# Six edits in a decoder step: loads of set-up rows, a root, bias products, attention's projections, the convolution's taps, its state output

## The chip, the cores and the metric

The kernel runs on one core of a Trainium2 chip. The metric is device time in microseconds (us) of one execution; lower is better. The core's engines run side by side, each through its own list of instructions in order: TensorE (PE) multiplies, VectorE (DVE), ScalarE (ACT) and GpSimd (POOL) work on elements, and SyncE (SP) mostly issues transfers (DMA). They wait for each other through semaphores.

## What is computed

One inference step of a trunk of four layers over 512 prompt tokens and 8 sample tokens, 1024 channels, in float32. Layers 0 and 3 mix tokens by causal pooling, layer 1 by dilated window attention in three groups, layer 2 by a convolution module; a SwiGLU feed-forward follows each. Cut to the main lines:

```python
def pool_mixer(h, hist, n_past, w_grp, scale):
    # trailing means over 2, 4, 8, 16 positions minus the token, a linear map per channel group, a scale
    ...
def conv_mixer(h, hist, w_in, b_in, w_dw, b_dw, ln_g, ln_b, w_out, b_out):
    a = h @ w_in + b_in
    u = a[..., :D_MODEL] * jax.nn.sigmoid(a[..., D_MODEL:])
    uh = jnp.concatenate([hist.astype(u.dtype), u], axis=1)
    c = lax.conv_general_dilated(uh, w_dw[:, None, :], (1,), 'VALID', ..., feature_group_count=D_MODEL) + b_dw
    ...
    z = (cf - mu) * lax.rsqrt(var + LN_EPS) * ln_g + ln_b
    y = jax.nn.silu(z).astype(h.dtype) @ w_out + b_out
    return y, uh[:, -CONV_HIST:]
...
for i in range(DEPTH):
    ...
    xp = xp + rmsnorm(mixer(rmsnorm(xp, norm_g[i, 0])), norm_g[i, 1])
    xp = xp + rmsnorm(swiglu(rmsnorm(xp, norm_g[i, 2]), w_ffn_in[i], w_ffn_out[i]), norm_g[i, 3])
```

The sample tokens pass through the same layers. The states (last 15 pooling inputs, window keys and values, last 30 convolution inputs) are outputs too.

## The kernel before

**Tiling.** Channels lie on partitions in eight blocks of 128, tokens along the free dimension: columns CA = 0 to 263 (8 sample tokens, 256 prompt tokens) and CB = 264 to 519. A product in float32 is made from parts: a weight is cast to a short float (`wh`, on ACT, L362) and its rest is `wl` (on DVE, L363), an activation likewise into `mh` and `ml`; three matmuls (L391, L392, L393 in `mm3`) give one term. A weight tile of 128 x 1024 (512 KB) is loaded on SP's queue (L352) into one of three `raw` tiles.

**Norms.** `pre_sums` adds the squares of eight blocks into `acc`; `rstat` turns them into a reciprocal root: L178 sums over partitions on PE, L180 takes the root on ACT (with a table load ahead), L183 the reciprocal on DVE, L185 spreads it on PE; `pre_r` (L338) copies it. Each engine's order is set by a scheduler that issues what its own model holds ready, unless the code names what an instruction must stand behind: `behind` does that, and `ROOT_FIRST` says for a sublayer and a column half how many weight casts after a root must stand behind it. The sublayers are numbered 0 to 7 (`self.at`).

**Start.** `load` issues on SP, in order: two x tiles, the pool's bands, eight groups of set-up rows into one tile (norm gains, biases, the 31 rows of `conv_w_dw`), the sample, the pool's state, x tiles 2 and 3. Then `pool` loads its weights (pool_w). `vectors` turns the rows onto partitions (L136) and the sample (L140), pooling means (L613) follow, then products with pool_w. Semaphores for SP's transfers are taken in turn from a set of eight, so a transfer's issue waits for the one eight before it. L544 sums the squares of the x tiles, L558 and L559 make their reciprocal root, L596 casts the sample's part.

**Attention.** Eight head pairs. `attend` is a generator: at each `yield` a budget of `FILL_STEPS` = 72 pieces of projections for the next head pair is dealt out over `ATT_STEPS` places, so that PE has work while softmax runs elsewhere. The lines between weights and values:

```python
        a = self.attn_weights(own)
        next(smp)
        for _ in range(4):
            yield
```

`attn_weights` merges the three groups (POOL copies L965 and L966, DVE L969 to L980, ACT L1006); `attn_values` begins with transposes of the weighted scores (L1012), later ones wait for `tl` (L1017) at L1033.

**Convolution sublayer.** `depthwise_setup` puts the taps together with 32 copies on POOL (L1215, L1216) into `conv_w` and `conv_b`; `depthwise` multiplies them with an identity of 32 columns into `dg` tiles (DVE, L1233) and runs the taps as matmuls (L1239). `sum_blocks` sums the result over channels (L1274), `conv_out` transposes and stores the state (L1264, L1265, L1266), `layer_norm` centres (L1287), squares (L1289, L1292), adds (L1293), scales (L1302, L1304), takes silu (L1305) and splits into `mh` and `ml` (L1307, L1308), and `linear_out` runs the output product, two weights' terms in turn. Hooks are generators that feed-forward sublayers step through beside their products; `conv_state` is one, in `ffn(1)`, the sublayer ahead.

## Time and profile before

| | us |
|---|---|
| median of 3 runs (2581.84 to 2587.22) | 2582.05 |
| profiled execution | 2584.28 |
| its span | 2582.5 |
| PE busy | 2491.2 (96%) |
| DVE busy | 1614.3 (63%) |
| ACT busy | 1229.2 (48%) |
| POOL busy | 449.5 (17%) |

The mean granted TensorE clock was 0.983 of full. The span begins at 0; times in the rows are from there. A wait is idle time of an engine just before an instruction, put down to what released it last by the trace; where that had long been done, it was another.

### The profile page before, as it was taken

Reading aid. Unit: us, or ns where it says so; the run is one execution under the profiler, and the core shown is the slowest. Engines: PE = TensorE matmul, PEld = TensorE weight load, DVE = VectorE, ACT = ScalarE, POOL = GpSimd, SP = SyncE. Lnnn points to the kernel's source line nnn. Section 1 sums busy time; section 2 is a strip of 40 time slices with the busy share of each in tenths; the row PEclk is TensorE's granted clock in tenths of the full one; section 3 lists DMA queues with packets and bytes.
Section 4 is the critical chain, followed back from the end, with each engine's and each line's share of the span. In section 5 each row is a group of like instructions: output and inputs, shape, how many; then the busy total and the mean of one; then the engine's idle time right before and its main releaser. Section 6 shows DMA issues by size and latency. Waiting matters only on the chain.

```text
span 2582.5 us, 51526 instructions
## 1 busy us (share of the span) xinstructions
PE 2491.2 (96%) x20832; PEld 2457.6 (95%) x20832; DVE 1614.3 (63%) x2906; ACT 1229.2 (48%) x2336; POOL 449.5 (17%) x747
## 2 busy tenths in 40 slices
PE   7999999999999999889999999989999998999998
PEld 7899999999999999889999989979999998999998
DVE  5745655667767777677474576467656557747564
ACT  6644434455544545555342353476444336635342
POOL 3100001222333322320000047322000005100002
PEclk8999999999999999999999999989999999999999
DMA  5585543444444554456464421036655432656451
GB/s 147 151 223 158 165 138 108 142 122 142 142 129 129 144 144 128 131 157 180 140 186 116 139 74 42 2 93 172 183 147 164 140 115 69 170 155 180 131 165 58
DMA packets 653435, 349.83 MB, mean 135 GB/s; under 512 B 14864, under 2 KB 649729, under 8 KB 652909
## 3 DMA queue, kind: packets, MB, share of 16 engines
q1 hardware_dynamic: 648996, 338.10, 45.6%
q0 software_dynamic: 1232, 6.06, 0.8%
q8 instruction: 164, 2.69, 0.5%
q10 hardware_dynamic: 2969, 2.37, 0.4%
q14 instruction: 74, 0.61, 0.1%
HBM read 331.87 MB, written 20.68 MB: 137 GB/s over the span
## 4 chain that ended last, share of the span: by engine, by line
PE 46%; POOL 2%; ACT 1%; DVE 1%; DMA 1%; issue 1%; DVEq 0%; ACTq 0%; POOLq 0%; SPq 0%
PE mm L391 14%; PE mm L392 14%; PE mm L393 14%; PE mm L1239 2%; POOL x L238 1%; DMA raw<-in_w_ffn_in_dram 1%; POOL acc L221 1%; POOL conv_w L1215 0%; PE mm L185 0%; ACT wh L362 0%; DVE wl L363 0%; PE mm L1274 0%; ACT sq L220 0%; PE mm L178 0%; DVE ml L317 0%
## 5 line engine op out<-in xcount | busy, mean ns | idle before, releaser
L391 PE MATMUL mm<-mh,wh 128*128 128x264 f32 (+1 forms) x4544 | 1309.7, 290 | 14.5 <-ACT mh L316 5.1
L392 PE MATMUL mm<-ml,wh 128*128 128x264 f32 (+1 forms) x4544 | 1293.8, 285 | 5.1 <-DVE ml L317 4.7
L393 PE MATMUL mm<-mh,wl 128*128 128x264 f32 (+1 forms) x4544 | 1290.0, 284 | 0.7 <-DVE wl L363 0.7
L362 ACT CAST wh<-raw 128x1024 fp32r<-128x1024 f32 (+1 forms) x557 | 573.9, 1036 | 657.7 <-PE mm L392 408.1
L391 PEld LDWEIGHTS mm<-mh,wh 128*128 128x128 f32 x4544 | 864.4, 191 | 20.5 <-ACT mh L316 6.7
L392 PEld LDWEIGHTS mm<-ml,wh 128*128 128x128 f32 x4544 | 867.1, 191 | 8.8 <-DVE ml L317 8.4
L393 PEld LDWEIGHTS mm<-mh,wl 128*128 128x128 f32 x4544 | 865.5, 191 | 1.0 <-DVE wl L363 1.0
L363 DVE TENSOR_TENSOR wl<-raw,wh 128x1024 fp32r<-128x1024 f32 (+1 forms) x557 | 682.0, 1229 | 282.8 <-ACT wh L362 277.3
L391 PE MATMUL mm<-h,wh 128*128 128x264 f32 (+1 forms) x1408 | 399.1, 283 | 0.9 <-DVE pr L1149 0.9
L392 PE MATMUL mm<-h,wh 128*128 128x264 f32 (+1 forms) x1408 | 398.3, 283 | 0.6 <-DVE h L420 0.6
L393 PE MATMUL mm<-h,wl 128*128 128x264 f32 (+1 forms) x1408 | 398.5, 283 | 0.0
L221 POOL TENSOR_TENSOR acc<-acc,sq 128x264 f32<-128x264 f32 (+1 forms) x90 | 79.3, 881 | 1385.8 <-ACT sq L220 1382.7
L391 PEld LDWEIGHTS mm<-h,wh 128*128 128x128 f32 x1408 | 265.7, 189 | 1.7 <-issue 1.3
L392 PEld LDWEIGHTS mm<-h,wh 128*128 128x128 f32 x1408 | 265.7, 189 | 1.1 <-DVE h L420 0.8
L393 PEld LDWEIGHTS mm<-h,wl 128*128 128x128 f32 x1408 | 265.7, 189 | 0.1
L417 DVE TENSOR_TENSOR u<-mm,r 128x264 f32<-128x264 f32 (+1 forms) x176 | 74.9, 426 | 85.4 <-PE mm L393 85.4
L238 POOL TENSOR_TENSOR x<-x,xt 128x264 f32<-128x264 f32 (+1 forms) x111 | 98.1, 908 | 85.3 <-DVE xt L233 83.5
L415 DVE TENSOR_TENSOR g<-mm,r 128x264 f32<-128x264 f32 (+1 forms) x176 | 74.9, 426 | 43.4 <-PE mm L393 39.7
L454 DVE TENSOR_TENSOR y<-mm,y 128x264 f32<-128x264 f32 x64 | 24.0, 429 | 124.5 <-PE mm L393 124.5
L1106 POOL TENSOR_TENSOR skv<-skv,lg 128x576 f32<-128x576 f32 (+1 forms) x48 | 52.7, 1133 | 218.1 <-ACT lg L1099 218.1
L927 ACT ACTIVATE x<-x,own 128x256 f32<-128x256 f32 (+1 forms) x128 | 61.9, 485 | 60.0 <-DVE own L926 60.0
L418 DVE TENSOR_TENSOR u<-u,g 128x264 f32<-128x264 f32 (+1 forms) x176 | 75.7, 434 | 22.7 <-ACT g L416 9.2
(224 smaller groups left out, 2506.6 us busy)
## 6 DMA issues: line engine op xcount, KB each, us to landing
raw<-in_w_ffn_in_dram SPq DMA_DIRECT2D x352, 512.0 KB
raw<-in_w_qkv_dram SPq DMA_DIRECT2D x72, 512.0 KB
raw<-in_w_ffn_out_dram SPq DMA_DIRECT2D x64, 512.0 KB
skv<-in_cache_swa_g_dram SPq DMA_DIRECT2D x32, 512.0 KB
raw<-in_w_ffn_out_dram SPq DMA_DIRECT2D x32, 384.0 KB
out_dram<-tm SPq DMA_DIRECT2D x32, 256.0 KB
raw<-in_conv_w_in_dram SPq DMA_DIRECT2D x16, 512.0 KB
skv<-in_cache_swa_g_dram SPq DMA_DIRECT2D x16, 256.0 KB
```

The lines of the kernel that those rows point to most:

```text
L221: (eng or nc.vector).tensor_add(post[c], post[c], sq)
L238: self.added = nc.gpsimd.tensor_add(xb, xb, t)
L362: whi = nc.scalar.copy(wh, raw)
L363: self.parted = whi, nc.vector.tensor_sub(wl, raw, wh.bitcast(F32))
L391: nc.tensor.matmul(ps, wh[:, k, :], mh, start=first, stop=False)
L392: nc.tensor.matmul(ps, wh[:, k, :], ml, start=False, stop=False)
L393: nc.tensor.matmul(ps, wl[:, k, :], mh, start=False, stop=last)
L415: nc.vector.tensor_mul(g, pg[2 * i], rr[c])
L417: nc.vector.tensor_mul(u, pg[2 * i + 1], rr[c])
L418: nc.vector.tensor_mul(u, u, g)
L927: nc.scalar.activation(pc, pc, AF.Exp, scale=-1.0, bias=stat[:, lay, 0, c:c + 1], accum_out=stat[:, lay, 1, c:c + 1])
L1106: nc.gpsimd.tensor_mul(v4[:, :, h, :], v4[:, :, h, :], lg[:, h, o:o + n, None].to_broadcast([128, n, 64]))
```

## The change

1. **Set-up rows.** The 31 rows of `conv_w_dw` are loaded as 16 and 15. The pool's state and pool_w are issued ahead of x tiles 2 and 3.
2. **Root.** `ROOT_FIRST` gets (1, CB): 4, the second half of the first feed-forward sublayer.
3. **Bias products.** In `bias_setup` the three matmuls are written ahead of the three copies.
4. **Attention.** Five places instead of four between weights and values, `ATT_STEPS` 28 instead of 27. From a head pair's last scores to its first transposes PE now has 108 projection matmuls, before 96; from its beginning 180, before 174. For the last head pair it is 96, before 84.
5. **Taps.** They are put together in `ffn(1)` by a hook behind `conv_state`: two halves, each a memset and 32 smaller copies on POOL into a side tile, then stored by POOL's queue in a DRAM tile `taps`. The convolution loads that with one transfer (128 x 1184, 592 KB) on SP. The bias is column 36 of the same tile. On SP that load stands behind the sixth weight of the sublayer.
6. **State output.** `conv_out` stands behind the last sum of CA, and the layer norm's first part is written ahead of it.

```diff
--- before.py
+++ after.py
@@ -39,8 +39,8 @@
 SQUARES_ON_POOL = {(1, CA): (2, 4, 6), (6, CA): (1, 3, 5, 7)}
 NEAR_END = {1: (), 4: (3,), 5: (2, 3, 6, 7)}
 STEPS = {4: (8, 0, 0, 0)}
-ROOT_FIRST = {(2, CB): 2, (7, CB): 4}
-ATT_STEPS, FILL_STEPS = 27, 72
+ROOT_FIRST = {(1, CB): 4, (2, CB): 2, (7, CB): 4}
+ATT_STEPS, FILL_STEPS = 28, 72
 LAST_STEPS = (1, 3, 5, 11)
 CONV_FILL = {(1, CB): 3, (2, CA): 3, (2, CB): 3, (3, CA): 3, (3, CB): 2}
 SLOTS = ((0, 0, 9), (1, 9, 9), (2, 18, 5))
@@ -120,14 +120,11 @@
             (R_G, I["norm_g"].rearrange("l f d -> (l f) d")), (R_PS, I["pool_scale"]),
             (R_BIN, I["conv_b_in"].rearrange("o (t d) -> (o t) d", t=2)), (R_BDW, I["conv_b_dw"]),
             (R_LNG, I["conv_ln_g"]), (R_LNB, I["conv_ln_b"]), (R_BOUT, I["conv_b_out"]),
-            (R_DW, I["conv_w_dw"].rearrange("o t d -> (o t) d")),
+            (R_DW, I["conv_w_dw"][0, 0:16, :]), (R_DW + 16, I["conv_w_dw"][0, 16:31, :]),
         ):
             nc.sync.dma_start(rows[r0:r0 + ap.shape[0], :], ap)
         nc.sync.dma_start(xs, I["x_sample"].rearrange("b o d -> (b o) d"))
         history = self.pool_history(0)
-        next(history)
-        for t in range(2, 4):
-            nc.sync.dma_start(self.xin[t], I["x_prompt"][0, t * 128:(t + 1) * 128, :])
         self.vec = c.tile([128, NB, NR], F32, name="vec")
 
         def vectors():
@@ -482,7 +479,10 @@
             for t in range(2):
                 self.load_tokens(t)
             begin[0]()
+            next(begin[1])
             st["w"] = weights()
+            for t in range(2, 4):
+                nc.sync.dma_start(self.xin[t], I["x_prompt"][0, t * 128:(t + 1) * 128, :])
         nc.vector.tensor_mul(sg, self.vec[:, :, R_PS + j], self.vec[:, :, post_row])
         self.flush()
         norm_after = 3 if begin else 1
@@ -757,6 +757,7 @@
         ps = self.psum(16, 368)
         for g, o, n in SLOTS:
             nc.tensor.matmul(ps[:, 16 * o:16 * (o + n)], rb[:, 16 * g:16 * g + 16], e2[:33, 16 * o:16 * (o + n)], start=True, stop=True)
+        for g, o, n in SLOTS:
             nc.scalar.copy(so.rearrange("h (k s) -> h k s", k=16)[:, :, o:o + n],
                            ps[:, 16 * o:16 * (o + n)].rearrange("h (k s) -> h k s", k=16))
         nc.scalar.dma_start(self.strip[:, 896:1264], so)
@@ -901,7 +902,7 @@
         yield from self.scores_g12(hp, kv, own, pr[1])
         a = self.attn_weights(own)
         next(smp)
-        for _ in range(4):
+        for _ in range(5):
             yield
         for i, _ in enumerate(self.attn_values(hp, kv, pr, a)):
             if i in (LAST_STEPS if last else (4, 7, 10, 13)):
@@ -1157,7 +1158,10 @@
         self.ul = lp.tile([128, NB, 32], F32, name="conv_ul")
 
         self.u2 = [lp.tile([128, 4, 8 + 128], F32, name=f"conv_u2{i}") for i in range(4)]
-        self.depthwise_setup(lp)
+        self.w2 = lp.tile([128, NB, 4, 37], F32, name="conv_w2")
+        nc.sync.dma_start(self.w2, self.taps)
+        for u2 in self.u2:
+            nc.gpsimd.memset(u2[:, :, 0:8], 0.0)
         rr, ub = {}, {}
         sums = [self.sum_blocks(c) for c in (CA, CB)]
         fill = chain(*(self.depthwise(lp, b) for b in range(NB)))
@@ -1192,28 +1196,34 @@
         for s in sums:
             for _ in range(7):
                 next(s)
-        self.conv_out(j)
         norm = [self.layer_norm(c, s) for c, s in zip((CA, CB), sums)]
+        next(norm[0])
+        with self.behind((self.summed,)):
+            self.conv_out(j)
         for _ in norm[0]:
             pass
         post = self.post(lambda b: self.v(post_row, b))
         self.linear_out(I["conv_w_out"][j], post, next_row, bias_row=R_BOUT, between=norm[1])
 
-    def depthwise_setup(self, lp):
+    def depthwise_setup(self):
+
 
         nc = self.nc
-        self.w2 = lp.tile([128, NB, 4, 36], F32, name="conv_w2")
-        self.b2 = lp.tile([128, NB, 4], F32, name="conv_b2")
-        self.id32 = lp.tile([128, 32], F32, name="conv_id")
+        self.id32 = self.const.tile([128, 32], F32, name="conv_id")
         nc.vector.tensor_reduce(self.id32, self.ident.rearrange("p (b k) -> p k b", b=4), axis=AX.X, op=ALU.add)
-        nc.gpsimd.memset(self.w2, 0.0)
-        for u2 in self.u2:
-            nc.gpsimd.memset(u2[:, :, 0:8], 0.0)
-        for p in range(4):
-            for q in range(4):
-                pp, pq = slice(32 * p, 32 * p + 32), slice(32 * q, 32 * q + 32)
-                nc.gpsimd.tensor_copy(self.w2[pp, :, q, 5 - p:36 - p], self.vec[pq, :, R_DW:R_DW + 31])
-                nc.gpsimd.tensor_copy(self.b2[pp, :, q], self.vec[pq, :, R_BDW])
+        self.taps = self.dram.tile([128, NB, 4, 37], F32, name="taps")
+        for hb in (slice(0, 4), slice(4, 8)):
+            w2 = self.side_tile()[:, :592].rearrange("p (b q k) -> p b q k", b=4, q=4)
+            nc.gpsimd.memset(w2, 0.0)
+            yield
+            for p in range(4):
+                for q in range(4):
+                    pp, pq = slice(32 * p, 32 * p + 32), slice(32 * q, 32 * q + 32)
+                    nc.gpsimd.tensor_copy(w2[pp, :, q, 5 - p:36 - p], self.vec[pq, hb, R_DW:R_DW + 31])
+                    nc.gpsimd.tensor_copy(w2[pp, :, q, 36], self.vec[pq, hb, R_BDW])
+                yield
+            nc.gpsimd.dma_start(self.taps[:, hb], w2)
+            yield
 
     def to_phases(self, b, ub):
 
@@ -1231,7 +1241,7 @@
         for q in range(4):
             d = lp.tile([128, 36, 32], F32, tag="dg", name=self.n("dg"), bufs=6)
             nc.vector.tensor_mul(d, self.id32[:, None, :].to_broadcast([128, 36, 32]),
-                                 self.w2[:, b, q, :, None].to_broadcast([128, 36, 32]))
+                                 self.w2[:, b, q, 0:36, None].to_broadcast([128, 36, 32]))
             dg.append(d)
         ps = self.psum()
         for q in range(4):
@@ -1244,7 +1254,7 @@
         for q in range(4):
             for s in range(4):
                 src = ps[32 * s:32 * s + 32, q * 128:q * 128 + 128].rearrange("c (h n) -> c h n", h=2)
-                dst, bias = yb[32 * q:32 * q + 32, :, 3 - s, :], self.b2[32 * s:32 * s + 32, b, q:q + 1]
+                dst, bias = yb[32 * q:32 * q + 32, :, 3 - s, :], self.w2[32 * s:32 * s + 32, b, q, 36:37]
                 if b >= 6 and s % 2:
                     nc.vector.tensor_scalar(dst, src, bias, None, op0=ALU.add)
                 else:
@@ -1271,7 +1281,7 @@
         for b in range(NB):
             if b == 0:
                 ps = self.total[c] = self.psum(128, hi - lo)
-            self.nc.tensor.matmul(ps, self.ones, self.y[:, b, lo:hi], start=b == 0, stop=b == 7)
+            self.summed = self.nc.tensor.matmul(ps, self.ones, self.y[:, b, lo:hi], start=b == 0, stop=b == 7)
             yield
 
     def layer_norm(self, c, sums):
@@ -1412,7 +1422,7 @@
         net.ffn(0, 3, 4)
     net.attn(5, 6)
     with net.phase(4, 4):
-        net.hooks.append(net.conv_state(0))
+        net.hooks.append(chain(net.conv_state(0), net.depthwise_setup()))
         net.ffn(1, 7, 8)
     net.conv(2, 0, 9, 10)
     with net.phase(4):
```

Three places in the engines' orders. SP at the start, behind the other rows (side_111 is the rows' tile, side_112 the sample, h_110 the x tiles). Before:

```order
L125 DMA side_111<-in_conv_w_dw_dram 31x1024
L126 DMA side_112<-in_x_sample_dram 8x1024
L522 DMA side_126<-in_state_pool_dram 120x1024
L130 DMA h_110<-in_x_prompt_dram 128x1024 x2
L352 DMA raw_188<-in_pool_w_dram 128x8x128
L352 DMA raw_194<-in_pool_w_dram 128x8x128
```

Now:

```order
L125 DMA side_111<-in_conv_w_dw_dram 16x1024
L125 DMA side_111<-in_conv_w_dw_dram 15x1024
L126 DMA side_112<-in_x_sample_dram 8x1024
L522 DMA side_185<-in_state_pool_dram 120x1024
L349 DMA raw_187<-in_pool_w_dram 128x8x128
L349 DMA raw_193<-in_pool_w_dram 128x8x128
L485 DMA h_110<-in_x_prompt_dram 128x1024 x2
```

The rows come in two pieces, and x tiles 2 and 3 moved behind pool_w.

ACT around the root of the first feed-forward sublayer's CB (wh are casts of weights, g and h the gate and its product). Before:

```order
L416 ACTIVATE g_965<-g_965 128x264
L362 CAST wh_1282<-raw_1280 128x1024
L419 CAST h_756<-u_966 128x264
L362 CAST wh_1288<-raw_1286 128x1024
L362 CAST wh_1294<-raw_1292 128x1024
L362 CAST wh_1300<-raw_1298 128x1024
L180 ACT_TABLE_LOAD
L180 ACTIVATE sd_1172<-mm_1171,eps_rms 128x2
```

Now:

```order
L413 ACTIVATE g_966<-g_966 128x264
L416 CAST h_757<-u_967 128x264
L177 ACT_TABLE_LOAD
L177 ACTIVATE sd_1173<-mm_1172,eps_rms 128x2
L359 CAST wh_1283<-raw_1281 128x1024
L335 COPY r_1181<-mm_1172 128x256
L359 CAST wh_1289<-raw_1287 128x1024
L359 CAST wh_1295<-raw_1293 128x1024
```

The root's table load and root moved ahead of the four casts; the fourth now stands nine rows further on.

PE at the beginning of the convolution's output product (mm_20842 and mm_20843, now mm_20881 and mm_20882, are the results of two weights). Before:

```order
L185 MATMUL mm_20769<-ident,rd_20777 128x8
L391 MATMUL mm_20842<-mh,wh_20832 128x264
L391 MATMUL mm_20843<-mh,wh_20838 128x264
L392 MATMUL mm_20842<-ml,wh_20832 128x264
L393 MATMUL mm_20842<-mh,wl_20833 128x264
L392 MATMUL mm_20843<-ml,wh_20838 128x264
L393 MATMUL mm_20843<-mh,wl_20839 128x264
```

Now, at the passage from the first weight to the second:

```order
L388 MATMUL mm_20881<-mh,wh_20871 128x264
L389 MATMUL mm_20881<-ml,wh_20871 128x264
L390 MATMUL mm_20881<-mh,wl_20872 128x264
L388 MATMUL mm_20882<-mh,wh_20877 128x264
L389 MATMUL mm_20882<-ml,wh_20877 128x264
L390 MATMUL mm_20882<-mh,wl_20878 128x264
```

The two weights' terms were taken in turn; now 24 of the first come ahead of 24 of the second.

ACT at the same place (20877 is the second weight, xt and mh the last blocks of the norm). Now:

```order
L1315 ACTIVATE xt_20857<-xt_20857,vec 128x264
L1315 ACTIVATE xt_20863<-xt_20863,vec 128x264
L1317 CAST mh<-xt_20857 128x264
L1317 CAST mh<-xt_20863 128x264
L359 CAST wh_20877<-raw_20875 128x1024
```

The second weight's cast stood ahead of the first silu; now it stands behind the last block.

## Rows read from the trace of the kernel before

**Rows 1.** The page, part 1: busy time, share of the span, instructions.

```profile
PE 2491.2 (96%) x20832; PEld 2457.6 (95%) x20832; DVE 1614.3 (63%) x2906; ACT 1229.2 (48%) x2336; POOL 449.5 (17%) x747
```

**Rows 2.** Waits of PE, whole span: line, releaser, total us, times, longest.

```profile
PE mm L185 <- DVE rd L183: 16.6, 9, 6.0
PE mm L136 <- DMA raw<-in_pool_w_dram: 9.3, 1, 9.3
PE mm L1012 <- ACT x L1006: 8.8, 7, 1.6
PE mm L178 <- DVE acc L1293: 7.1, 2, 6.6
...
PE mm L178 <- DVE acc L331: 4.1, 1, 4.1
PE mm L391 <- ACT mh L1307: 3.9, 1, 3.9
...
PE mm L391 <- DVE mh L596: 1.4, 1, 1.4
...
PE mm L1033 <- DVE tl L1017: 1.0, 2, 0.8
```

**Rows 3.** Stretches: length, busy us (instructions) by engine, granted clock, DMA share, GB/s.

```profile
108.50:115.40 6.90, 5.29 (x25) 5.29 (x26) 5.78 (x11) 6.01 (x9) 0.00 (x0) 0.51 0.75 221
115.40:130.00 14.60, 14.60 (x123) 14.42 (x123) 9.60 (x20) 7.78 (x14) 0.00 (x0) 1.00 0.40 114
...
1525.20:1532.00 6.80, 6.76 (x33) 6.75 (x34) 5.80 (x14) 3.46 (x9) 4.50 (x6) 0.51 0.01 2
...
1698.00:1702.60 4.60, 4.19 (x19) 4.19 (x20) 4.51 (x13) 4.60 (x13) 0.00 (x0) 0.50 0.38 114
```

**Rows 4.** Timeline at the start: start us, length us, instruction, idle before.

```profile
4.81 1.06 ACT L544 ACTIVATE h<-h 128x1024 f32<-128x1024 f32 x1 [2.11 <-DMA h<-in_x_prompt_dram]
...
7.67 0.23 SPq L125 DMA_DIRECT2D side<-in_conv_w_dw_dram  x1
...
17.91 1.07 PE L136 MATMUL mm<-ident,side 55*128 55x55 f32 x8 [9.30 <-DMA raw<-in_pool_w_dram]
```

**Rows 5.** Waits of SP's queue from 0 to 32 us.

```profile
SPq L352 <- DMA side<-in_conv_w_dw_dram: 0.2, 1, 0.2
```

**Rows 6.** Timeline, first feed-forward sublayer, root of CB.

```profile
101.20 0.50 PE L178 MATMUL mm<-ones,acc 128*128 128x2 f32 x4
...
107.24 1.04 ACT L362 CAST wh<-raw 128x1024 fp32r<-128x1024 f32 x1 [1.21 <-DMA raw<-in_w_ffn_in_dram]
108.30 1.28 ACT L180 ACT_TABLE_LOAD   x1
...
110.11 1.22 PE L185 MATMUL mm<-ident,rd 128*128 128x128 f32 x4 [5.96 <-DVE rd L183]
```

**Rows 7.** Timeline, attention, one head pair.

```profile
687.77 3.56 POOL L966 COPY oth<-own 32x4 f32<-32x4 f32 x16
...
695.28 0.84 PE L1012 MATMUL mm<-ident,x 128*128 128x128 f32 x4 [1.53 <-ACT x L1006]
```

**Rows 8.** Timeline, end of the feed-forward sublayer, start of the convolution.

```profile
1504.41 0.28 PE L393 MATMUL mm<-h,wl 128*128 128x256 f32 x1
...
1510.11 1.21 DVE L363 TENSOR_TENSOR wl<-raw,wh 128x1024 fp32r<-128x1024 f32 x1
...
1510.28 1.29 POOL L1215 COPY conv_w<-vec 32x248 f32<-32x248 f32 x1
...
1515.38 0.38 POOL L1215 COPY conv_w<-vec 32x248 f32<-32x248 f32 x1
...
1519.22 1.36 DVE L1233 TENSOR_TENSOR dg<-conv_id,conv_w 128x1152 f32<-128x1152 f32 x1 [3.94 <-POOL conv_w L1215]
```

**Rows 9.** Timeline, layer norm ahead of the convolution's output product.

```profile
1683.81 1.45 DVE L1287 SCALAR_TENSOR_TENSOR y<-mm,y 128x264 f32<-128x264 f32 x4 [2.15 <-PE mm L1274]
...
1694.59 1.04 ACT L362 CAST wh<-raw 128x1024 fp32r<-128x1024 f32 x1 [0.38 <-DMA raw<-in_conv_w_out_dram]
```

## The prediction

> **What bounds the kernel now.** I read the page's busy shares first: TensorE (PE) is busy for 96% of the span [rows 1], so time can only be won where PE stands still or runs at the lower clock, and work on another engine costs something only if PE waits for it. The second view is the list of PE's waits over the whole span [rows 2]. Six of its rows answer to places that the diff edits: the 9.3 us at L136 (set-up rows), the longest 6.0 us of L185 (a root in the first feed-forward sublayer), the 8.8 us at L1012 (seven of attention's eight head pairs), the 4.1 us at L178 for L331 (start of the convolution sublayer), and the 7.1 (longest 6.6) and 3.9 us at L178 and L391 for L1293 and L1307 (the layer norm ahead of the convolution's output product). The third is the table by stretches, with the granted clock [rows 3]. There a wait shows its second price. Right after the 6.0 us wait PE runs at a clock of 0.51 of full, the 1.2 GHz level: 25 matmuls take 5.29 us of work, where the next stretch, at 2.4 GHz, does 123 in 14.60 us, 0.119 us each. Those 25 would have taken 3.0 us, so 2.3 us went to the clock. After the 4.1 us wait it is 33 in 6.76 us, 2.8 us over 33 x 0.119. A wait removed there may give the clock's part back too.
>
> **The change part by part.**
>
> *A, set-up rows.* PE starts L136 at 17.91 us after a wait of 9.30 [rows 4]. The page names a pool_w load, but what it needs is the rows' tile: its last piece, the 31 rows of conv_w_dw (124 KB), was issued at 7.67 [rows 4], and SyncE's queue was still waiting for exactly that transfer just ahead of its issue at 17.6 [rows 5]. So 124 KB took about 9.9 us, while an x tile of 512 KB, issued at 0.75 as the queue's first, is there at 4.81 [rows 4]. In 16 and 15 rows the two pieces are issued by about 8.2. Bounds: if a piece's time goes by its rows, each takes 5 us and the rows are there at 13.2, a gain of 4.7; if they land like other transfers, in 2 to 4 us, they are there at 10.2 to 12.2, a gain of 5.7 to 7.7. I take 10.5, that is 7, since the x tile is eight times the size of a piece and takes 4.
> The Trainium skill ("DMA: Bandwidth & Descriptors", section "Why a DMA increments its semaphore by 16 and not by 1") has a rule for the number of DMA engines: the largest number up to 16 that divides the slowest dimension of both sides, so 31 rows go to one engine and 16 and 15 rows to 16 and 15. By that rule the faster bound holds; the 9.9 us of the trace agree with one engine, and no row here shows a transfer of 15.
> What hides less afterwards: state_pool and the pool weights now go ahead of x tiles 2 and 3. The product behind the pooling, which before waited 1.4 us for L596 [rows 2], now has its reciprocal for those tiles (L559) ahead of L596 on VectorE, so it can start only when the tiles are in. No wait before names them; now 2 MB, four transfers of 512 KB, must be in by the time that the means are done. A = 7, bounds 4 to 8.
>
> *B, the root ahead of the weight casts.* The sums of L178 run at 101.20 for 0.50 us; ScalarE (ACT) does the square root's table load only at 108.30, for 1.28 us, because four casts stand ahead of it in its order and those wait for their loads (the last 1.21 us, at 107.24); PE goes on at 110.11 after 5.96 us [rows 6]. Now the root stands ahead of the four casts. At the latest its table load begins when the sums end, at 101.7: 1.28 for the load, 0.3 for the root, some 0.3 for VectorE's reciprocal give 103.6. PE stopped at 110.11 - 5.96 = 104.15, and its L182 stands four matmuls earlier now, 103.7. So the wait goes, 5.96, and the clock's 2.3 with it. The casts come behind the root; two were waiting for loads anyway, and PE has the products of weights cast before. If two casts are late by a cast each, 2 x 1.04 us come back. B = 8, bounds 5 to 8.3.
>
> *C, bias products.* Three matmuls no longer wait behind a copy of the one ahead. No row of [rows 2] names that line. Up to one copy each might have held PE: 0.3, bounds 0 to 1.
>
> *D, one more place for projections.* In each of eight head pairs the wait is at the first transposes, L1012. It ends with a chain on GpSimd: 16 copies of L966 from 687.77 for 3.56 us, then VectorE and ACT, then PE at 695.28 [rows 7]. That chain hangs on scores far back. Between the last scores and these transposes 96 projection matmuls stood, now 108; counted from the beginning of a head pair it is only 6 more, since the budget went from 27 to 28. If the chain is fixed to the head pair's beginning, each wait shrinks by 6 x 0.119 = 0.71; if to the last scores, by up to 1.43. The last head pair has no later work to draw on, so I count seven: 7 x 0.71 = 5.0. The upper bound is 8.8, all that these waits hold. The lower is 3: later places have 6 matmuls fewer to cover L1033, which waits 1.0 us now [rows 2].
>
> *E, taps put together earlier.* GpSimd's 32 copies at the convolution's start go; the diagonal of L1233 waited 3.94 us for them and started at 1519.22 [rows 8], and behind it the sums that PE awaited for 4.1 [rows 2]. Now one load of 606 KB brings the taps. It stands behind six weights of the sublayer and behind the last h product, which ends near 1504.7 [rows 8]; with the x tile's 4 us for 512 KB [rows 4] and other loads beside it, it lands by 1511, against the 1515.3 at which VectorE was ready (1519.22 less the wait). So the 4.1 goes. Of the 2.8 us of slow clock behind it I count 2, because VectorE is then next: it was busy for 5.80 of 6.80 us in that stretch [rows 3]. E = 6, bounds 3 (the taps or the pushed-back weights late by 3) to 7.
> Where the 32 copies now run, beside the feed-forward sublayer, they meet VectorE's weight work. The trace: a copy of L1215 takes 0.38 us alone and 1.29 when begun just behind a VectorE operation of 1.21, which itself isn't stretched [rows 8]. A copy that comes second waits; the other way round VectorE would lose at most a copy's 0.38.
> The Trainium skill ("SBUF — State Buffer", section "SBUF: two separate sides") has this as a lock: of a GpSimd operation and a VectorE operation with two SBUF inputs, the second to start is blocked for the whole of the first. The trace agrees for the copy; no row shows the reverse. By that rule this part has a price of its own, which is the third rival.
>
> *F, state output behind the sums.* Before, 16 transposes and four copies of the state stood ahead of the last sums; VectorE's first centring began at 1683.81, and a weight's casts (one of 1.04, after a wait for its load, at 1694.59) and splits stood inside the chain to the first product [rows 9]. Now the last sum of CA comes ahead of the transposes, about 1.4 us sooner, and all casts but one stand behind the chain: I put the first product 3.5 us sooner (2 to 4). But the two weights' products are no longer taken in turn. Before, each block of mh and ml fed six matmuls; now 24 of the first weight come, then 24 of the second, whose cast stands behind ACT's last block. ACT does 13 operations in 4.60 us there, fully busy [rows 3]; two are needed per block, so blocks come every 0.7 to 0.8 us, and a block's three matmuls are done in 0.36. The first 24 take some 6.2 us, then the cast, 1.04, and the split, 1.21 like that of [rows 8], lie open, then 22 more matmuls, 2.6: 11.1 us. Before, 19 of the 48 took 4.2 us at the low clock [rows 3] and 29 x 0.119 = 3.5, 7.7. So 3.4 is lost against 3.5 won, and the next pair of weights is loaded later, since the queue now waits for the state's output: about 2 more. F = -2, bounds -5 to +1.5.
>
> **The sum.** 7 + 8 + 0.3 + 5 + 6 - 2 = 24.3 us. The profiled execution took 2584.28 us (span 2582.5 and 1.8 around it); 2560.0 is left. The median of before, 2582.05, lies 2.2 us lower, so I forecast 2582.05 - 24.3 = 2557.8, **2558 us**. With bounds that don't all fall on one side: 2549 to 2567.
>
> **Rivals.**
> 1. *The waits move rather than go*: A's product waits for x tiles behind 2 MB (A = 4), and D's chain shifts with the scores (D = 0). 24.3 - 3 - 5 = 16.3, 2566. For it: everything on GpSimd's chain starts from scores. Against: six matmuls really move ahead. Chance 0.13.
> 2. *More comes back than counted*: D at 8.8, F at +1.5, C at 1: 24.3 + 3.8 + 3.5 + 0.7 = 32.3, 2550, and 2547 with A and B at their upper bounds (1 + 0.3) and 2 more of the clock. For it: slow-clock stretches follow several of these waits. Chance 0.08.
> 3. *The taps' copies hold VectorE*: 32 x 0.38 = 12.2 us if every copy came first and PE felt it. VectorE has spare time in that stretch, and buffers lie between. 2558 + 12 = 2570. Chance 0.04.
> 4. *Slower*: in attention the later places run short. If L1033 waits 1.4 us (the 12 matmuls moved) in each of eight head pairs, and each wait brings a slow stretch like those above, 2.3 us, that is 8 x 3.7 = 30 us, and D's 5 are lost: 2558 + 35 = 2593. It decides when that wait passes the length that brought the low clock elsewhere. Against it: L1033 waits 1.0 us in all, so there is slack. Chance 0.03.
> 5. *The change doesn't do what it says*: 31 rows aren't what L136 waits for and root and taps are still behind a load: 2558 + 7 + 8 + 6 = 2579. Chance 0.02.
>
> **How the numbers follow.** The forecast has 0.70; 2547 to 2569 takes in most of rivals 1 and 2. A measurement of this kernel can tell about 0.2%, 5 us, from no change: faster means below 2576.9. Only rivals 4 and 5 lie outside that: faster 0.94, same 0.03, slower 0.03.
>
> **What would show it.** A: L133 near 10.5, products near 22.5. B: no wait above 1 us at L182 near 104, full clock behind. D: the first L1013 waits 0.7 shorter in each head pair. E: the diagonal not waiting, no 4 us at L175. F: products of the first weight every 0.8 us, and a wait for the second's cast. I am wrong if L133 still waits for a load, if the taps land later than VectorE is ready for them, or if waits at L1033's place grow.

## The result and the profile of the changed kernel

The changed kernel takes 2602.50 us (median of 6 runs, 2600.88 to 2603.54), the kernel before, run beside it, 2586.88 (6 runs, 2581.84 to 2588.27): a ratio of 1.0065 [1.0052, 1.0078]. The change makes the kernel slower by 0.65%, where 1% less was forecast. The profiled execution took 2603.29 us against 2584.28 of before, 19.0 more, over a span of 2601.5. These 19.0 are what has to be explained, and with them the 24.3 that were to be won.

PE's waits over the whole span of the changed kernel (what waited, what released it, sum in us, number, longest), in the order of their size:

```profile
PE mm L873 <- DVE t L863: 24.8, 7, 4.4
PE mm L388 <- ACT mh L313: 13.6, 5, 9.5
PE mm L182 <- DVE rd L180: 11.5, 9, 2.9
PE mm L175 <- DVE acc L1303: 4.8, 2, 4.3
...
PE mm L388 <- ACT mh L1317: 3.6, 1, 3.6
PE mm L873 <- DVE srd L1119: 3.4, 1, 3.4
PE mm L175 <- POOL acc L218: 3.4, 1, 3.4
...
PE mm L133 <- DMA side<-in_x_sample_dram: 2.6, 1, 2.6
PE mm L388 <- DVE mh L596: 2.1, 1, 2.1
```

Beside [rows 2]: the 9.3 us of the set-up rows (L136, now L133) are 2.6, the root's 6.0 (the longest at L185, now L182) is gone (the longest of that row, 2.9, stands elsewhere), of the 4.1 at the convolution's start 0.5 is left, and of the 8.8 at L1012 (now L1013) 0.2 is left. The waits that the change aimed at did go. In their place stand two that [rows 2] does not have at this size: 24.8 us at L873, a transpose in attention, and, at the beginning of the second feed-forward sublayer, one of 9.5 at L388 with one of 3.4 at L175 behind it.

Where the time lies is seen by the same matmul in both traces: each kernel has 20832 of them, in the same order but for local changes, and the table gives by how much the one with the given number starts later (+) or sooner (-) than in the profiled execution of before. The lower rows are the experiments of the next section.

| us, by place in before | 71 (rows) | 127 (root) | 178 (bias) | 527 | 1052 (attention's end) | 1096 | 1157 (FFN begun) | 1473 | 1532 (conv begun) | 1580 | 1813 | end |
|---|---|---|---|---|---|---|---|---|---|---|---|---|
| after | -7.9 | -16.5 | -13.7 | -15.2 | **+7.2** | +10.1 | **+24.1** | +22.7 | +14.5 | +16.0 | +20.2 | +19.2 |
| x_rows | -9.4 | -9.8 | -11.3 | -12.8 | -13.5 | -10.5 | -10.7 | -11.9 | -12.8 | -12.4 | -10.4 | -10.4 |
| x_ab | -7.6 | -16.2 | -8.4 | -10.0 | -10.9 | -9.1 | -7.9 | -9.1 | -10.0 | -9.8 | -7.4 | -3.5 |
| x_nod | -7.2 | -15.8 | -12.6 | -14.1 | -10.9 | -11.8 | +4.9 | +2.1 | -6.2 | -4.8 | -2.8 | -3.8 |
| x_d | -0.6 | -0.3 | -1.8 | -2.9 | +17.5 | +20.6 | +20.7 | +21.3 | +21.0 | +21.0 | +20.8 | +20.8 |
| x_noe | -5.7 | -14.3 | -9.0 | -10.5 | +10.4 | +10.2 | +10.8 | +9.9 | +10.0 | +10.0 | +12.1 | +11.0 |
| x_fixe | -6.8 | -15.4 | -11.5 | -13.0 | -13.5 | -10.7 | -9.4 | -11.0 | -18.6 | -17.1 | -15.2 | -16.2 |
| x_nof | -7.7 | -16.3 | -13.0 | -14.5 | +8.6 | +8.3 | +24.1 | +21.4 | +13.1 | +14.7 | +16.5 | +16.4 |
| x_abce | -8.4 | -17.0 | -14.1 | -15.7 | -17.1 | -14.0 | -14.1 | -15.7 | -23.8 | -22.2 | -21.1 | -22.6 |
| x_abcde | -6.4 | -15.0 | -10.7 | -12.2 | -8.0 | -6.7 | -6.5 | -7.3 | -15.4 | -14.0 | -13.9 | -15.5 |
| x_best | -4.4 | -13.0 | -9.9 | -11.4 | -13.1 | -13.4 | -12.1 | -13.3 | -21.0 | -19.6 | -17.7 | -18.7 |
| x_bestf | -8.1 | -16.7 | -12.4 | -13.4 | -14.1 | -14.2 | -13.8 | -15.4 | -23.3 | -21.9 | -20.8 | -20.8 |

In the first row the start wins 16.5 us and keeps 15.2 up to attention. Attention loses 22.4, the beginning of the feed-forward sublayer 14.0, the convolution's beginning wins 8.2, and the layer norm's stretch loses about 4; the other steps are 3 us or less each. x_best and x_bestf have the same code up to 1580 us and differ by 3.7 in the first column, so a single difference below some 4 us is not taken as shown unless several kernels have it.

**The start** (answers [rows 4, 6]). The timeline of the changed kernel, start and length in us, idle time before in brackets:

```profile
7.36 0.78 SPq L125 DMA_DIRECT2D side<-in_conv_w_dw_dram  x2
...
10.29 0.67 PE L133 MATMUL mm<-ident,side 55*128 55x55 f32 x8 [2.63 <-DMA side<-in_x_sample_dram]
...
92.25 1.28 ACT L177 ACT_TABLE_LOAD   x1
...
93.78 0.26 ACT L177 ACTIVATE sd<-mm,eps_rms 128x2 f32<-128x2 f32 x1 [0.25 <-PE mm L175]
93.94 1.04 ACT L359 CAST wh<-raw 128x1024 fp32r<-128x1024 f32 x1
```

The two pieces of the rows, issued by 8.1, are used at 10.29. The root's table load is done before the sums are (ACT idles 0.25 us for them), and the cast comes behind the root.

**Attention** (answers [rows 7]). First the stretch from the 527 us column to the 1052 one, as a table of busy times: of before, then of the changed kernel. The columns are the stretch, its length, PE, PEld, DVE, ACT and POOL busy (instructions), the granted clock, the DMA share, GB/s.

```profile
527.00:1052.00 525.00, 513.33 (x4636) 500.81 (x4635) 368.54 (x822) 268.85 (x645) 161.39 (x322) 0.99 0.47 134
```

```profile
512.00:1059.00 547.00, 518.84 (x4633) 508.74 (x4634) 366.92 (x824) 270.75 (x648) 161.92 (x322) 0.98 0.45 129
```

PE stands idle for 547.00 - 518.84 = 28.2 us where it was 11.7: 16.5 more. It is also busy for 5.5 more with the same matmuls (but for three at the edges), at a lower clock. Together 22.0, the loss of the stretch but for 0.4. The 28.2 us are two rows of the list of waits, 24.8 and 3.4, both at L873. In one head pair the changed kernel's timeline has:

```profile
678.38 3.57 POOL L967 COPY oth<-own 32x4 f32<-32x4 f32 x16
...
681.98 0.17 DVE L970 TENSOR_TENSOR cm<-own,oth 128x16 f32<-128x16 f32 x1 [6.93 <-POOL oth L967]
...
682.37 0.42 DVE L863 TENSOR_TENSOR t<-mm,r 128x256 f32<-128x256 f32 x1
...
682.84 0.33 PE L873 MATMUL mm<-ident,t 128*128 128x128 f32 x1 [3.39 <-DVE t L863]
...
684.17 0.41 PE L389 MATMUL mm<-ml,wh 128*128 128x256 f32 x1
684.38 0.41 PE L390 MATMUL mm<-mh,wl 128*128 128x256 f32 x1
```

`t` is the next head pair's projection times its norm (0.42 us of VectorE), and L873 transposes it. It stands on VectorE behind three operations of the merge, L970 to L972, and the first of these idles for 6.93 us until GpSimd's copies are done. The same place in before:

```profile
682.69 0.40 DVE L862 TENSOR_TENSOR t<-mm,r 128x256 f32<-128x256 f32 x1
...
684.39 0.41 DVE L862 TENSOR_TENSOR t<-mm,r 128x256 f32<-128x256 f32 x1
691.37 0.17 DVE L969 TENSOR_TENSOR cm<-own,oth 128x16 f32<-128x16 f32 x1 [6.56 <-POOL oth L966]
```

There both multiplications for `t` were ahead of the merge. VectorE idled about as long (6.56), but nothing that PE needed sooner than the merge's own result was behind the idle instruction. After the wait PE's matmuls start 0.21 us apart (684.17, 684.38) instead of 0.119 [rows 3]: from 684.17 to 686.00 the granted clock is 0.50, the 1.2 GHz level, and it is 0.76 over the row

```profile
684.00:690.00 6.00, 6.00 (x41) 6.00 (x41) 5.96 (x16) 4.32 (x10) 0.00 (x0) 0.76 0.52 151
```

Such stretches behind the seven waits are where the 5.5 us go.

**The second feed-forward sublayer begins** (no row of before stands for it). Changed kernel; the stretch as a row of the table of busy times, and the timeline:

```profile
1120.00:1130.00 10.00, 0.61 (x5) 0.40 (x4) 2.04 (x4) 0.47 (x2) 9.09 (x32) 0.69 0.27 86
```

```profile
1116.13 2.37 POOL L235 TENSOR_TENSOR x<-x,xt 128x264 f32<-128x264 f32 x2
1118.45 0.48 POOL L1222 COPY side<-vec 32x124 f32<-32x124 f32 x1
...
1127.41 0.61 POOL L1225 DMA_DIRECT2D taps<-side  x1 [0.30 <-POOL side L1223]
...
1128.77 2.41 POOL L235 TENSOR_TENSOR x<-x,xt 128x264 f32<-128x264 f32 x3
1129.53 0.52 ACT L313 ACTIVATE mh<-x,vec 128x264 fp32r<-128x264 f32 x1 [10.17 <-POOL x L235]
...
1130.10 0.81 PE L388 MATMUL mm<-mh,wh 128*128 128x264 f32 x2 [9.49 <-ACT mh L313]
```

For ten microseconds hardly anything but GpSimd works (9.09 us of 10): it puts taps together. The first half's copies and their store stand, in its order, between the fifth and the sixth of the eight residual additions (L235) that end the attention sublayer for CA. Those additions give `x`; ACT splits it, and PE, which had begun the feed-forward product with the blocks that were there, stands still for 9.49 us until it has the next. The whole stretch, 1096 to 1157 us of before and the same matmuls in the changed kernel, in the columns of the table of busy times:

```profile
1096.00:1157.00 61.00, 54.29 (x408) 52.17 (x407) 48.20 (x89) 35.12 (x70) 18.43 (x22) 0.94 0.53 154
```

```profile
1106.10:1181.10 75.00, 57.65 (x408) 55.16 (x408) 46.21 (x88) 35.66 (x70) 37.29 (x90) 0.86 0.46 134
```

PE idles 17.35 us instead of 6.71, 10.6 more, and is busy for 3.4 more with the same 408 matmuls, at a granted clock of 0.86 instead of 0.94. That is the 14.0.

**The convolution begins** (answers [rows 8]). Changed kernel:

```profile
1527.96 0.92 SPq L1162 DMA_DIRECT2D conv_w<-taps  x1
...
1536.61 1.33 DVE L1243 TENSOR_TENSOR dg<-conv_id,conv_w 128x1152 f32<-128x1152 f32 x1
```

No idle time stands before the diagonal now, and the table shows 8.2 us won between 1473 and 1532.

**The layer norm** (answers [rows 9]). PE's waits at L175 are 4.8 (before 7.1) and at L388 3.6 (before 3.9). The first matmul of the output product stood at 1698.41 in before, which is 1714.4 by the table's +16.0 at 1580; the timeline of the changed kernel has it sooner:

```profile
1711.92 0.59 PE L388 MATMUL mm<-mh,wh 128*128 128x264 f32 x1 [3.55 <-ACT mh L1317]
...
1719.32 0.39 PE L390 MATMUL mm<-mh,wl 128*128 128x264 f32 x1 [0.75 <-DVE wl L360]
```

So 2.5 us are won up to the first product, and lost again behind it, at the second weight's split among others.

### The profile page after: what moved, and what is told of

It reads as the page before. It is cut to its first block, busy times and chain, and to the rows that moved or that the text cites. A ratio compares the mean times of both kernels' runs of the same rounds, so it can differ in the third digit from the quotient of the medians.

```text
span 2601.5 us, 51555 instructions
## 1 busy us (share of the span) xinstructions
PE 2499.9 (96%) x20832; PEld 2466.8 (95%) x20832; DVE 1609.9 (62%) x2906; ACT 1229.1 (47%) x2336; POOL 454.0 (17%) x782
## 3 DMA queue, kind: packets, MB, share of 16 engines
q10 hardware_dynamic: 2969, 2.37, 0.4%
## 4 chain that ended last, share of the span: by engine, by line
PE 77%; POOL 8%; ACT 4%; DVE 4%; DMA 4%; issue 2%; SPq 1%; POOLq 0%; ACTq 0%; DVEq 0%
PE mm L388 23%; PE mm L389 23%; PE mm L390 23%; PE mm L1249 2%; POOL skv L1076 2%; DMA raw<-in_w_ffn_in_dram 2%; POOL x L235 1%; DVE wl L360 1%; ACT wh L359 1%; POOL oth L966 1%; POOL acc L218 1%; POOL oth L967 1%; PE mm L1013 1%; DMA bias<-bias_full 1%; PE mm L182 1%
## 5 line engine op out<-in xcount | busy, mean ns | idle before, releaser
L388 PE MATMUL mm<-mh,wh 128*128 128x264 f32 (+1 forms) x4544 | 1311.5, 290 | 23.8 <-ACT mh L313 13.6
L388 PEld LDWEIGHTS mm<-mh,wh 128*128 128x128 f32 x4544 | 867.3, 191 | 30.4 <-ACT mh L313 15.5
L388 PE MATMUL mm<-h,wh 128*128 128x264 f32 (+1 forms) x1408 | 399.6, 284 | 1.9 <-DVE u L414 1.1
L388 PEld LDWEIGHTS mm<-h,wh 128*128 128x128 f32 x1408 | 266.3, 189 | 2.6 <-DVE u L414 1.4
L235 POOL TENSOR_TENSOR x<-x,xt 128x264 f32<-128x264 f32 (+1 forms) x111 | 97.4, 902 | 91.0 <-DVE xt L230 89.3
L863 DVE TENSOR_TENSOR t<-mm,r 128x256 f32<-128x256 f32 x144 | 80.9, 564 | 23.4 <-PE mm L390 23.3
```

Source lines behind the costliest of these rows:

```text
L235: self.added = nc.gpsimd.tensor_add(xb, xb, t)
L388: nc.tensor.matmul(ps, wh[:, k, :], mh, start=first, stop=False)
L863: nc.vector.tensor_mul(d, f(src), f(rv))
```

## The experiments

Edits A to F are the six of the prediction's text: rows, root, bias products, place in attention, taps, state output. Three kernels take A in part: x_rows, x_best and x_bestf split the rows but leave the loads in their order of before.

**D undone.** The changed kernel without the fifth place:

```diff
-ATT_STEPS, FILL_STEPS = 28, 72
+ATT_STEPS, FILL_STEPS = 27, 72
...
-        for _ in range(5):
+        for _ in range(4):
```

> The changed kernel with the projection places put back (four places, 27 steps), the rest of the change kept. Theory 1: the 4 us waits at the lone transposes of the next head pair's projections come from VectorE's order, in which one of the two multiplications that make t now stands behind the merge of the three groups, and the merge waits for GpSimd's copies. With four places both stand ahead of it again, so seven waits of 2.7 to 4.4 us at L873 go, the seven of about 1.5 us at the first L1013 come back, the 3.4 us at L1034 in the last head pair go: about 24 us less than the changed kernel, 8 us below the kernel before. Rival: the waits come from the rows and the root having moved everything some 16 us earlier against the transfers; then they stay at L873 and the time stays within 3 us of the changed kernel's, 16 us above before.

Measured: 2581.27 us, ratio to before 0.9987 [0.9974, 1.0]; by the ratios the changed kernel is 20 us slower than this. PE's waits:

```profile
PE mm L388 <- ACT mh L313: 14.3, 6, 9.5
...
PE mm L1013 <- ACT x L1007: 7.4, 6, 1.7
```

No row at L873 for `t`, the old waits at L1013 are back, attention costs 3.2 us in the table where the changed kernel costs 22.4. The 9.5 of L388 is still there, so it does not come from D.

**D alone.** The kernel before with that edit only:

```diff
-ATT_STEPS, FILL_STEPS = 27, 72
+ATT_STEPS, FILL_STEPS = 28, 72
...
-        for _ in range(4):
+        for _ in range(5):
```

> The kernel before with five places and 28 steps and nothing else. Theory 1: the cost doesn't hang on the rest of the change: seven waits of 3 to 4.5 us at L872's lone transpose, one near 3.5 at L1033 in the last head pair, 20 to 25 us above before. Rival: the waits need the earlier start or the earlier root; then within 6 us of before, and 5 us below it if the prediction's term held.

Measured: 2604.94 us, 1.0070 [1.0054, 1.0086]. PE's waits:

```profile
PE mm L872 <- DVE t L862: 23.7, 7, 4.2
```

The same wait, and nearly all of the 20.8 us are lost within attention (-2.9 to +17.5): D's loss does not depend on the other edits.

**E undone.** The changed kernel with `depthwise_setup` at the convolution's start, as before:

```diff
-        net.hooks.append(chain(net.conv_state(0), net.depthwise_setup()))
+        net.hooks.append(net.conv_state(0))
...
-        nc.sync.dma_start(self.w2, self.taps)
+        self.depthwise_setup(lp)
```

> The changed kernel with the taps put together at the convolution's start as before, the rest kept. Theory 1: the wait of 9.5 us at L388 and of 3.4 us at L175 in the second feed-forward sublayer come from the 64 tap copies on GpSimd, which stand ahead of the residual adds there. Without them 14 us come back there, and 7 to 8 us are lost again at the convolution's start: 6 us less than the changed kernel, 10 us above before. Rival: those waits follow from the late end of attention and stay; then 7 us slower than the changed kernel, 23 us above before.

Measured: 2599.87 us, 1.0045 [1.0030, 1.0060]. PE's waits:

```profile
PE mm L873 <- DVE t L863: 23.2, 7, 4.0
...
PE mm L388 <- ACT mh L313: 5.8, 6, 2.2
...
PE mm L175 <- DVE acc L328: 4.1, 1, 4.1
```

Between 1096 and 1157 it loses 0.6 instead of 14.0, and between 1473 and 1532 it wins nothing instead of 8.2. E is a gain of 8 and a loss of 14 (16.7 in x_nod, 15.8 in x_nof, which have the same order on GpSimd).

**E in another order on GpSimd.** The changed kernel without D, and with each half's memset, hence all its copies, behind the last residual addition:

```diff
-            nc.gpsimd.memset(w2, 0.0)
+            with self.behind((self.added,)):
+                nc.gpsimd.memset(w2, 0.0)
```

> The changed kernel with the projection places put back and the memset ahead of the tap copies issued behind the last residual add on GpSimd, so that the copies can't stand in front of those adds. Theory 1: the 14 us at the start of the second feed-forward sublayer are owed to the copies' place in GpSimd's order alone; they go, the 8 us at the convolution's start stay won: about 16 us less than with the places put back alone, 18 to 20 us below before. Rival: the copies hold GpSimd or VectorE wherever they run; then at least half of the 14 us shows up later in that sublayer.

Measured: 2567.55 us, 0.9926 [0.9906, 0.9946], by the ratios 16 us less than x_nod. GpSimd's timeline:

```profile
1113.43 5.07 POOL L235 TENSOR_TENSOR x<-x,xt 128x256 f32<-128x256 f32 x6 [7.28 <-DVE xt L230]
...
1119.04 0.61 POOL L1218 MEMSET side<- 128x592 f32 x1
```

And PE's waits:

```profile
PE mm L388 <- ACT mh L313: 5.3, 6, 2.0
```

The additions run through, then the taps begin. The same copies, in the same sublayer, now cost 1.3 us between 1096 and 1157, and the 7.6 at the convolution's start stay. It was their place, not their work.

**F undone.** The changed kernel with `conv_out` ahead of the last sums, as before:

```diff
+        self.conv_out(j)
         norm = [self.layer_norm(c, s) for c, s in zip((CA, CB), sums)]
-        next(norm[0])
-        with self.behind((self.summed,)):
-            self.conv_out(j)
```

> The changed kernel with the state's output ahead of the last sums as before, the rest kept. Theory 1: the output product takes the two weights' terms in turn again and the next weights are in time: 2 to 5 us less than the changed kernel, 11 to 14 us above before. Rival: the layer norm's chain, shortened by the move, gains more than the product loses: 2 us or more slower than the changed kernel.

Measured: 2599.83 us, 1.0050 [1.0035, 1.0065], 2.7 below the changed kernel with intervals that overlap. From 1580 to 1813 it loses 1.8, the changed kernel 4.2. But x_nod, x_noe and x_fixe, which have F too, lose 2.0, 2.1 and 1.9 there, no more than x_nof; and x_abce, which is x_fixe without F, loses 1.1, its median 4.2 below x_fixe's with intervals that overlap. So a cost of F is not shown; by these traces it lies between nothing and 2.4 us.

**F with the store on another queue.** x_best (below) with F, the state's output issued by GpSimd so that SyncE's weights don't wait for it:

```diff
-            nc.sync.dma_start(dst, o[skip:n, :])
+            nc.gpsimd.dma_start(dst, o[skip:n, :])
```

> As the run before it, and the state's output behind the sums as in the change, but stored through GpSimd's queue, so that SyncE's queue doesn't wait for it. Theory 1: the move costs by the weights of the output product coming later; with the queue free the two weights' terms go in turn after the first few and the earlier sums show: 1 to 3 us below the run before it. Rival: casts pushed behind the norm cost as much as before: same or up to 3 us above.

Measured: 2564.83 us, 0.9916 [0.9902, 0.9931], against 0.9915 [0.9897, 0.9933] of x_best: no difference that can be told. What F is worth with this store stays open, within a few us either way.

**Rows alone.** The kernel before with 16 and 15 rows, one execution:

```diff
-            (R_DW, I["conv_w_dw"].rearrange("o t d -> (o t) d")),
+            (R_DW, I["conv_w_dw"][0, 0:16, :]), (R_DW + 16, I["conv_w_dw"][0, 16:31, :]),
```

> Only the 31 set-up rows as 16 and 15; loads in the old order, the rest as before. If the rows' transfer was what PE waited for, L133 starts near 10.3 as in the changed kernel, and 5 to 8 us of the wait go. If the order of the other loads did it, L133 stays near 17.9.

Measured: 2573.76 us. Its timeline:

```profile
7.21 0.78 SPq L125 DMA_DIRECT2D side<-in_conv_w_dw_dram  x2
...
10.17 0.67 PE L136 MATMUL mm<-ident,side 55*128 55x55 f32 x8 [1.67 <-DMA side<-in_x_sample_dram]
```

PE begins at 10.17 as in the changed kernel, and 9.4 us are won by 71 us. The rows do it; the order of the other loads is not needed for that.

**Rows and root, without the bias products' order.** The kernel before with A, the loads' order, and B:

```diff
-ROOT_FIRST = {(2, CB): 2, (7, CB): 4}
+ROOT_FIRST = {(1, CB): 4, (2, CB): 2, (7, CB): 4}
```

> Only the set-up rows with the order of the loads, and the root ahead of four casts; the rest as before. Theory 1: each stands by itself, 8.0 and 8.6 us below before, 16.5 in all, and no waits of 4 us at L872 in attention. Rival: the gains at the start are taken back later by loads that are not earlier; then under 8 us.

Measured: 2578.77 us, 0.9961 [0.9948, 0.9975]. By its ratio it is about 10 ahead, where 16.5 was expected. It is 16.2 ahead at 127 us, like the other kernels with A and B (13.0 to 17.0), and then gives 7.8 back by 178 us, where the nine kernels that have C as well give back 2.8 to 5.3 (x_rows and x_d, without B and C, win 1.5 there). Another 3.9 go behind 1813 us, where no other kernel loses time; their cause was not followed. PE's waits from 130 to 180 us:

```profile
PE mm L759 <- ACT side L760: 6.4, 1, 6.4
```

And ACT's timeline there:

```profile
149.52 1.05 ACT L359 CAST wh<-raw 128x1024 fp32r<-128x1024 f32 x1 [1.35 <-DMA raw<-in_w_ffn_out_dram]
...
157.21 0.28 ACT L760 COPY side<-mm 16x144 f32<-16x144 f32 x1 [0.75 <-PE mm L759]
```

A bias product waits for the copy of the one ahead, and ACT's casts before that copy wait for weights that PE, 16 us earlier, now asks for sooner. In before, without A and B, PE has no such wait. In the nine kernels with C none stands there either.

**What gains, together.** The changed kernel without D and F, with E in the order above:

> As the run before it in this call, and the state's output as in the kernel before. Theory 1: the output product takes its two weights in turn, so the time is 0 to 3 us lower still, about 20 us below before. Rival: the move of the state's output is worth something once the rest is right; then 1 to 3 us higher.

Measured: 2563.36 us (2561.41 to 2569.08), 0.9918 [0.9896, 0.9940]: faster than the kernel before and the changed one. Its profiled execution is 22.9 below that of before, 22.6 at the last matmul; by the ratio it is 21.

**The same with the loads in their order of before** (x_best):

```diff
         history = self.pool_history(0)
+        next(history)
+        for t in range(2, 4):
+            nc.sync.dma_start(self.xin[t], I["x_prompt"][0, t * 128:(t + 1) * 128, :])
```

> Rows as 16 and 15 with the loads in the old order, the root ahead of four casts, bias products ahead, and the taps earlier with the copies behind the last residual add; places and state output as before. Theory 1: what of the change gains by itself, without its two costs; the loads in the old order start the first product 1 to 3 us sooner than with pool_w ahead of the x tiles: 23 to 26 us below before. Rival: pool_w ahead of the x tiles was worth something later; then no lower than 22 us below before.

Measured: 2566.49 us, 0.9915 [0.9897, 0.9933]. The ratios of the two are the same; what the order of the loads is worth can't be told from these runs.

**D with VectorE's order mended.** x_abce with five places, and with the merge's VectorE part written behind the last multiplication for `t`, one place ahead of the transposes:

```diff
-        a = self.attn_weights(own)
+        merge = self.attn_weights(own)
+        next(merge)
...
+        with self.behind((self.turned,)):
+            a = next(merge)
+        yield
```

> As the second run of this call, with five places and 28 steps, and the merge's VectorE part written one place ahead of the transposes and issued behind the last multiplication into t. Theory 1: the extra place costs only by VectorE's order; with t ahead of the merge the waits at L873 stay away and those of 1.5 us at the first transposes shrink: 3 to 8 us less than the second run. Rival: six matmuls fewer for the later places cost what the first ones win, at L1034 above all: within 2 us, or slower.

Measured: 2573.05 us, 0.9946 [0.9927, 0.9965], 9.7 above x_abce by the medians and 7 by the ratios, whose intervals overlap. PE's waits:

```profile
PE mm L1018 <- ACT x L1012: 12.0, 7, 2.7
...
PE mm L1039 <- DVE tl L1023: 4.7, 3, 4.0
```

The 24.8 at L873 for `t` are gone, and attention costs 4.2 in the table instead of 22.4. That shows the cause of D's loss: VectorE's order. But the transposes (now L1018) wait 12.0 us, where they wait 7.4 to 12.1 in the kernels with four places. So with this mend D brings nothing. The mend is not free of a price of its own: it holds the merge back on VectorE, and GpSimd's 16 copies for it, which take 3.56 us in a row in x_abce, take 4.94 here in one head pair, with single copies of up to 1.20 us where x_abce has none above 0.19. What D would bring without such a price is not shown.

## Why the prediction was wrong, and where it was right

**D is the step that failed first.** It was put at a gain of 5 and cost 22. The text followed one wait, L1012's, back to GpSimd and counted the matmuls between. It did not ask what else waits behind the same chain. Six matmuls moved ahead on PE bring their `t` multiplications to another place on VectorE, and VectorE takes its instructions in order: one of them fell behind L970, which idles for GpSimd in every head pair (56.0 us in eight, before 51.5). The 6.56 us of idle time of before cost PE nothing but the short waits at L1012, and the change put a product's input behind it. Rival 4 had the sign (2593, a chance of 0.03) and the place, attention, but not the mechanism: L1033's place, now L1034, waits 3.6 us in two places, not 1.4 in eight head pairs. Its other half, that each wait brings a stretch at the lower clock, holds in kind, with 5.5 us where it put 18. The counted gain of 5 was not seen either: in the changed kernel the wait at the transposes is down to 0.2, but PE has waited up to 4.4 ahead of it in the same head pair, and in x_abcde, where that wait is mended, it did not shrink. That would be rival 1's case for D (0), but the mend's own price stands in between.

**E failed in its second part.** At the convolution the step was right and a little small: 6 forecast, 8.2 measured. The load landed in time; the diagonal didn't wait. But the copies' new place was weighed only for what they do to VectorE (rival 3, 12.2 us at most, from the 32 copies of before where there are now 64 smaller ones). What stood next to them on GpSimd's own queue was not asked, and there the residual additions were, on PE's path: 14.0 us. x_fixe shows that the price was that of the order, but for the 1.3 us left.

**A and B were right.** A: L133 at 10.29 (forecast 10.5; it still waits 2.6 for the sample's load, which by its letter was one of the signs of being wrong), first products with pool_w at 24.04 (22.5; 2.1 of wait for L596 stand before), 7.9 won where 7 was forecast. The Trainium skill ("DMA: Bandwidth & Descriptors", section "Why a DMA increments its semaphore by 16 and not by 1") lets 31 rows use one engine and 16 and 15 rows use as many as they have rows; the trace agrees, as both pieces are in use 2.9 us after the first one's issue, where one piece of 31 rows took 9.9. B: between 71 and 127 us each kernel with B wins 8.6 (8 forecast).

**C was mis-sized.** 0.3 was forecast, since no wait named the line. With A and B in, the comparison of x_ab with the kernels that have C makes it 2.5 to 5, from one profiled execution of x_ab. A wait that isn't there in the trace of before appears when PE comes earlier.

**F is not settled.** A loss of 2 was forecast; it is 2.4 by the pair of x_nof and the changed kernel, and under 1 by the other kernels with F. The first product did come 2.5 sooner (3.5 forecast), and in the changed kernel this was lost again behind it, as forecast; how the loss divides was not measured.

**The sum.** A, B, C and E were to bring 21.3; x_abce, which has these four with E's order mended, is 22.6 ahead at its last matmul. So the terms for what was removed hold in the sum, in part by luck: A, B and E at the convolution bring 8.4, 8.6 and 8.1 in it, more than the 21 forecast, and 2.9 are lost again between 127 and 178 us. The result lies 44.5 us above the forecast of 2558: D is 27 of it (22 and the 5 not won), E's additions 14, and the kernel before itself was 4.8 higher beside it than in the runs that the forecast started from; the small differences of the other terms take 1 off again. The range of 2547 to 2569 had no room for either, because each edit's lower bound was made from the wait it touched and not from its neighbours on the other engines.

**Open.** The waits at L1034's place vary, from nothing in some kernels to 4.0 us in one place of x_abcde; why is not settled. Nor is all by which x_abcde is slower than x_abce: in the table it is 9.1 behind by attention's end. 3.5 of these are there before attention begins, where the two kernels are alike; of the other 5.6, PE's waits in attention are 4.5 (17.6 against 13.1). That the projections dealt earlier made the scheduler put `t` behind the merge was read from the two orders, and was not tried by itself.

## What to carry to other kernels

A step that is moved takes its place among others on every engine that it touches: look, on each of them, at which instruction stands ahead of it there and idles, and who waits for the one behind it. Long idle times of an engine with spare time are harmless only while nothing that the bottleneck needs is queued behind them; mark them before you move anything past them. And when several waits are removed at once, the later ones are met by an engine that comes earlier, so a wait that doesn't show before (a bias product's copy) may be the next.

## What the runs showed of the hardware

GpSimd's small copies are stretched by VectorE, and the reverse, which the prediction said no row shows, now has one: an operation of VectorE stretched beside GpSimd's. Both from the changed kernel's timeline in the second feed-forward sublayer:

```profile
1111.13 1.45 POOL L235 TENSOR_TENSOR x<-x,xt 128x264 f32<-128x264 f32 x2 [9.55 <-DVE xt L230]
...
1116.91 0.97 DVE L314 SCALAR_TENSOR_TENSOR ml<-x,vec,mh 128x264 fp32r<-128x264 f32 x1
...
1120.81 1.23 DVE L360 TENSOR_TENSOR wl<-raw,wh 128x1024 fp32r<-128x1024 f32 x1
1120.91 1.18 POOL L1223 COPY side<-vec 32x4 f32<-32x4 f32 x1
...
1130.08 0.49 DVE L314 SCALAR_TENSOR_TENSOR ml<-x,vec,mh 128x264 fp32r<-128x264 f32 x1 [8.03 <-ACT mh L313]
```

A copy of four columns takes 1.18 us when it begins 0.1 behind a VectorE operation of 1.23, and ends with it. VectorE's L314 took 0.97 us beginning inside the GpSimd additions of 1116.13 shown above, and 0.49 later. The Trainium skill ("SBUF — State Buffer", section "SBUF: two separate sides") has the second to start blocked by the first for its whole length; the copy agrees. VectorE's 0.97 agrees in kind only: the two additions beside it were themselves stretched (2.37 us, where two take 1.45 at 1111.13), and the rows don't tell who held whom for how long. This was not the price of E: as x_fixe shows, the same copies in another place cost 1.3 us between 1096 and 1157.
